# An mLSTM and attention trunk on one core: earlier down weights in the second MLP, and GpSimd sharing the conditioning sums

## The chip, the cores and the metric

The kernel runs on one core of a Trainium2 chip. The core has a matrix engine (TensorE, PE in the profile; its weight loads are listed as PEld), VectorE (DVE), ScalarE (ACT), GpSimd (POOL) and SyncE (SP), whose queue issues the transfers of this kernel. The metric is the device time of one execution in microseconds, as the median of several runs. Before the change it is 2478.76 us (three runs, 2478.34 to 2480.81).

## The reference

The reference is one inference step of a two-layer trunk over a prompt of 1024 rows and a sample of 32 rows, each 1024 wide. Both go through the same weights with their own state and their own conditioning vector `c`. Cut to what matters here:

```
def ada_mod(c, w, b):
    return jax.nn.silu(c) @ w + b
...
for l in range(DEPTH):                      # DEPTH = 2
    sh1, sc1, g1, sh2, sc2, g2 = split(ada_mod(c, w_ada[l], b_ada[l]), 6)
    u = x * (1 + sc1) + sh1
    y = mlstm_mixer(u, ...) if l == 0 else band_attention(u, ...)
    x = layer_norm(ALPHA * x + (1 + g1) * y)
    u = x * (1 + sc2) + sh2
    f = square(relu(u @ w_up[l])) @ w_down[l]     # 1024 -> 4096 -> 1024
    x = layer_norm(ALPHA * x + (1 + g2) * f)
```

So each layer needs six vectors of 1024 conditioning values, for two conditioning vectors (that of the prompt and that of the sample), and a further pair of vectors feeds the shared keys and values. Each is a product of a vector of 1024 with a matrix of 1024 columns. All results are float32. The kernel reaches that accuracy on PE by splitting each operand into a high part and the rest, and by three matmuls for each product (high by high, high by rest, rest by high).

## The kernel before, in words

Prompt and sample rows lie side by side as 1056 columns, in three blocks of 384, 384 and 288. Stage after stage, PE does the products: the first conditioning values and the mLSTM's projections with the mLSTM itself, up to about 480 us; the first MLP, up to about 1260; queries, keys, values and attention, up to about 1640; the output projection; the second MLP from about 1720 to the end. The kernel is written with a library that plans, from the order of the program and from estimated durations, in which order the instructions of an engine stand in its queue, and that puts in the waits. Two stretches have PE's order written out by hand: attention and the down stage of the second MLP (`manual_schedule`). An engine, SyncE among them, works through its queue in order.

The conditioning sums. The first 2048 columns of layer 0 are done on PE. All others are done by `ada_cols`, in pairs of 128-column blocks: `ada_l0` (16 pairs) runs beside the mLSTM, `ada_rest` (24 pairs of layer 1 and 8 for keys and values) beside the first MLP. A pair reads its weights in two halves (line 231), each with four chunks of 128 rows; for each chunk and each of the two vectors (`cnd` 0 and 1) VectorE multiplies 128x256 weights by one value per partition and adds the product to the sum `acc[:, cnd]` (line 238; the first one writes without adding, line 241). Then it transposes the sums (line 245), reduces them over 32 columns (line 246), and after each fourth pair PE finishes the sum over partitions. `ada_l0` has a single buffer, `ada_room`, with places for one half of the weights, for the sums and for the transposed sums; `ada_rest` takes its weights from the ring of three "raw" buffers that also receives the weights of the MLP (line 96), and its sums from the ring of five temporaries (`tmp_t`). The generators are fed forward by `flow.tick`, a few ticks per step, so that these sums lie among the other work.

The second MLP (`mlp7`). Its up stage runs in 16 blocks of 256 hidden columns. Blocks 0 to 13 are prepared for a product with fewer multiplications: each pair of quarters of the 1056 columns becomes seven operands, written to memory (`hd`, line 1170). Blocks 14 and 15 (`NW` and `NW + 1`) are taken plainly by `up_plain`: relu and square on ACT, the split into an `hl` tile, which is written to memory too (`hpl`, line 1191) for a last plain stage. For block 15 the `hl` tiles come from a pool of two buffers; for block 14 they come from the ring of three raw buffers.

The down stage then works in 16 units (four groups of blocks by four blocks of 256 output columns). A unit needs weights in seven forms, which `forms` makes from two loads (`rdn`, line 1228) into raw buffers, split and summed on ACT and VectorE (lines 89, 90, 1245 to 1248), and 14 operands `fx`, which `fill` reads back from `hd` into free rooms (line 1117). Rooms are four tiles `f4` at first; when block 15's up products no longer read one half of the MLP's input, that half's memory gives further rooms (`L.rooms(tp0)`, then `tp1`). `prep(i)` asks for the weights of unit `i`; each `next(preps[i])` makes one step of its forms. The order of the program between the up and the down stage is, before the change: rooms and the first operands, `up_plain` of block 14, `prep(0)`, `up_plain` of block 15's first half, the four steps of unit 0's forms, `prep(1)`, rooms and operands, `up_plain` of the second half, rooms and operands, and then the units, by hand, on PE (line 1283), with VectorE adding each result (line 986).

Of the kernel before, what the change touches and what calls it, by code (L numbers as in the profile page):

```python
# [9 lines left out]
F32R = mybir.dt.float32r  # L10
AF = mybir.ActivationFunctionType
ALU = mybir.AluOpType
# [3 lines left out]
P = 128  # L16
# [59 lines left out]
def trunk_kernel(ctx: ExitStack, tc: tile.TileContext, a, o):  # L76
    nc = tc.nc
# [3 lines left out]
    ring = ctx.enter_context(tc.tile_pool(name="ring", bufs=1, reuse_waits="tile"))  # L81
# [5 lines left out]
    def split(dst_h, dst_l, src, eng=None):  # L87

        nc.scalar.copy(dst_h, src)
        (eng or nc.vector).tensor_sub(dst_l, src, dst_h.bitcast(F32))  # L90
# [74 lines left out]
    def ada_part(l, i):  # L165
        return ada[:, l * 48 + i * KC:l * 48 + (i + 1) * KC, :]
# [10 lines left out]
    def tpt(name):  # L177
        return pa.tile([P, 512], F32, tag="tp", name=name, bufs=2)
# [27 lines left out]
    tp = tpt("tp_c")  # L206
# [13 lines left out]
    tp = tpt("tp_p2")  # L220
# [3 lines left out]

    def ada_cols(src, c0, base, nch, mk, tmp_f, step, raw_f=raw_tile):

        for j in range(0, nch, 2):
            acc = tmp_f([P, 2, 256], f"aacc_{base}_{j}")
            for half in range(2):
                raw = raw_f([P, 4, 256], f"rada_{base}_{j}_{half}")  # L230
                nc.sync.dma_start(raw, src[512 * half:512 * half + 512, c0 + j * P:c0 + (j + 2) * P].rearrange(
                    "(k p) c -> p k c", p=P))
                yield step[0]
                for k in range(4):
                    for cnd in range(2):
                        sc = cs[:, 4 * half + k, cnd:cnd + 1]
                        if half or k:
                            nc.vector.scalar_tensor_tensor(acc[:, cnd], raw[:, k], sc, acc[:, cnd],  # L238
                                                           op0=ALU.mult, op1=ALU.add)
                        else:  # L240
                            nc.vector.tensor_scalar(acc[:, cnd], raw[:, k], sc, None, op0=ALU.mult)
                    if k == 1 and step[1]:
                        yield step[1]
            at = tmp_f([P, 512], f"aat_{base}_{j}")
            nc.vector.transpose(at, acc.rearrange("p c n -> p (c n)"))
            nc.vector.tensor_reduce(out=cx[:, j // 2 % 4], in_=at.rearrange("p (b i) -> p b i", i=32), axis=mybir.AxisListType.X,
                                    op=ALU.add)
            yield step[2]
            if j // 2 % 4 == 3:
                ps = mk(f"adas_{base}_{j}")  # L250
                for q in range(4):
                    nc.tensor.matmul(ps[32 * q:32 * q + 32, :16], sel, cx.rearrange("p g b -> p (g b)")[:, q::4],
                                     start=True, stop=True)
                b0 = base + j - 6
                nc.vector.tensor_tensor(
                    ada[:, b0:b0 + 8, :].rearrange("p (g b) c -> p g b c", g=4),
                    ps[:, :16].rearrange("p (g c b) -> p g b c", g=4, c=2),
                    pt2[:, b0:b0 + 8].rearrange("p (g b) -> p g b", g=4)[:, :, :, None].broadcast_to([P, 4, 2, 2]),
                    op=ALU.add)

    def ada_fix(base, parts):

        for i, kind in parts:
            ap = ada[:, base + i * KC:base + (i + 1) * KC, :]
            if kind == "sc":
                nc.vector.tensor_scalar_add(ap, ap, 1.0)
            else:
                nc.vector.tensor_scalar(ap, ap, 1.0, 1.0 / ALPHA, op0=ALU.add, op1=ALU.mult)
# [461 lines left out]
    def ada_l0():  # L730
        room = ring.tile([P, 2112], F32, tag="wc", name="ada_room", bufs=6)

        def raw_f(shape, name):
            return room[:, 1024:2048].rearrange("p (k c) -> p k c", k=4)

        def tmp_f(shape, name):
            return room[:, 512:1024] if len(shape) == 2 else room[:, :512].rearrange("p (k c) -> p k c", k=2)
        yield from ada_cols(a["w_ada"][0], 2048, 16, 32, adat, tmp_f, ADA_C, raw_f)
        ada_fix(0, [(2, "g"), (4, "sc"), (5, "g")])
    flow.add(ada_l0())  # L740
# [56 lines left out]
    def tmp_t(shape, name, dt=F32):  # L797
        return T_.tile(shape, dt, tag="t", name=name, bufs=5)
# [290 lines left out]
    QN = T // 4  # L1089
    NPB, KG = 16, 4  # L1090
    NW = 14
# [32 lines left out]
    def mlp7(L):  # L1124
# [7 lines left out]
        l, mm = L.l, L.alloc  # L1132
# [14 lines left out]
        def up_mm(pb, f, q):  # L1147
            ps = mm(f"up{l}_{pb}_{f}_{q}")
            proj(ps[:, :QN], QN, up_w(pb), f, lambda hl, k: L.u(hl, k, q))
            return ps[:, :QN]  # L1150
# [29 lines left out]
        def up_plain(pb, tp):  # L1180
            for f in range(2):
                r = tmp_t([P, 2, QN], f"hr{l}_{pb}_{f}_{tp}")
                for i in range(2):
                    nc.scalar.activation(r[:, i], up_mm(pb, f, 2 * tp + i), AF.Relu)
                    flow.tick(QN / 96)
                nc.scalar.activation(r, r, AF.Square)
                name = f"hl{l}_{pb}_{f}_{tp}"
                hl = hlp.tile([P, 2, 2, QN], F32R, tag="hl", name=name, bufs=2) if pb == NPB - 1 else \
                    ring.tile([P, 2, 2, QN], F32R, tag="raw", name=name, bufs=3)
                split(hl[:, 0], hl[:, 1], r)  # L1190
                nc.sync.dma_start(hpl[2 * (pb - NW) + f, :, :, 2 * tp * QN:2 * (tp + 1) * QN],
                                  hl.bitcast(F32).rearrange("p l q t -> p l (q t)"))

        tp0, tp1 = L.pairs
# [24 lines left out]
        hlp = hl_cm.__enter__()  # L1219
# [75 lines left out]
        def prep(i):  # L1295
            if i < len(units):
                preps[i] = forms(*units[i][:2], f"{l}_{i}")
                next(preps[i])
        for t in f4:
            rooms.add(t)  # L1300
        want += [(tp, f) for tp in L.pairs for f in order_f]
        fill(0, fx)
        for tp in L.pairs:
            up_plain(NW, tp)
        prep(0)
        up_plain(NW + 1, tp0)
        for _ in range(4):
            got[0] = next(preps[0])
        prep(1)
        for t in L.rooms(tp0):  # L1310
            rooms.add(t)
        fill(0, fx)
# [53 lines left out]
    acc_cm, acc = open_acc(0, fwd)  # L1366
    mm, norm, _, out_proj, mlp, _, _ = make_layer(acc, bank, uap)
# [286 lines left out]
    with tc.manual_schedule(engines={mybir.EngineType.PE}):  # L1654
        for gp in range(2):
            for i in range(17):
                c = slim[gp][i // 2] if i % 2 else wide[i // 2] if i < 16 else slim[gp][8]
# [18 lines left out]
    acc = {ti: ACC[:, :, t0:t0 + n] for ti, (t0, n) in enumerate(TBS)}  # L1676
# [12 lines left out]
    def u2ap(hl, k, t0, n):  # L1689
# [5 lines left out]
    mm, norm, norm_out, out_proj, _, gain_shift, add_gated_at = make_layer(  # L1695
        acc, lambda name: psD.tile([P, 512], F32, tag="mm", name=name, bufs=8), u2ap, 2 * QN)
# [25 lines left out]
    class L1:  # L1722
        wups = wup1
        l, alloc, add, gate = 1, mm, add_gated_at, ada_part(1, 5)
# [74 lines left out]
```

## Time and profile before

| | |
|---|---|
| median of three runs | 2478.76 us (2478.34 to 2480.81) |
| the profiled execution | 2479.81 us, span 2478.0 us |
| PE busy | 2413.7 us, 97% of the span |
| VectorE busy | 1759.7 us, 71% |
| ScalarE busy | 1016.9 us, 41% |
| GpSimd busy | 168.6 us, 7% |
| mean granted clock of PE | 0.992 of full speed |

The profile is taken from one execution, by the chip. An instruction has the line of the program that issued it; many are issued by helpers, so that lines 118 to 120 are the matmuls of every plain product, and lines 89 and 90 the two halves of every split. Names such as `dn<-fx,wf` say which tile is written from which. "Idle before" is the time that an engine stood still just before an instruction, with what released it.

### The profile page before, as it was taken

Reading aid. Unit: us, or ns where it says so; the run is one execution under the profiler, and the core shown is the slowest. Engines: PE = TensorE matmul, PEld = TensorE weight load, DVE = VectorE, ACT = ScalarE, POOL = GpSimd, SP = SyncE. Lnnn points to the kernel's source line nnn. Section 1 sums busy time; section 2 is a strip of 40 time slices with the busy share of each in tenths; the row PEclk is TensorE's granted clock in tenths of the full one; section 3 lists DMA queues with packets and bytes.
Section 4 is the critical chain, followed back from the end, with each engine's and each line's share of the span. In section 5 each row is a group of like instructions: output and inputs, shape, how many; then the busy total and the mean of one; then the engine's idle time right before and its main releaser. Section 6 shows DMA issues by size and latency. Waiting matters only on the chain.

```text
span 2478.0 us, 42688 instructions
## 1 busy us (share of the span) xinstructions
PE 2413.7 (97%) x16844; PEld 2315.4 (93%) x16844; DVE 1759.7 (71%) x4038; ACT 1016.9 (41%) x2118; POOL 168.6 (7%) x315
## 2 busy tenths in 40 slices
PE   7999999999999999999999999999999999999997
PEld 4999999999999999999999867789999999899997
DVE  4899999788679679677597667746853442776758
ACT  4644456382211212212266556654754443221212
POOL 0211100000000000000001134410000000000003
PEclk9999999999999999999999989999999999999999
DMA  8433224313224224234122310050375646767632
GB/s 297 122 110 101 84 88 129 107 35 119 77 87 137 84 86 135 80 92 142 43 98 82 91 40 1 18 147 27 134 251 212 215 179 254 262 239 273 255 130 72
DMA packets 236220, 318.10 MB, mean 128 GB/s; under 512 B 11624, under 2 KB 185084, under 8 KB 234996
## 3 DMA queue, kind: packets, MB, share of 16 engines
q1 hardware_dynamic: 236020, 315.38, 38.8%
q8 instruction: 132, 2.16, 0.4%
q14 instruction: 68, 0.56, 0.1%
HBM read 242.79 MB, written 74.91 MB: 128 GB/s over the span
## 4 chain that ended last, share of the span: by engine, by line
PE 78%; DVE 8%; DMA 6%; ACT 2%; issue 1%; POOL 0%; SPq 0%; DVEq 0%; POOLq 0%; ACTq 0%
PE up L118 10%; PE up L120 10%; PE up L119 9%; PE dn L1283 9%; PE dn L119 5%; PE dn L118 5%; PE dn L120 5%; DMA fx<-hd 3%; PE pv L1608 2%; PE pt L1588 2%; PE s L1558 2%; PE o L118 1%; PE o L119 1%; PE o L120 1%; PE op_b L118 1%
## 5 line engine op out<-in xcount | busy, mean ns | idle before, releaser
L120 PE MATMUL up<-u,w_up 128*128 128x264 f32 x1024 | 292.9, 286 | 0.0
L118 PE MATMUL up<-u,w_up 128*128 128x264 f32 x1024 | 292.4, 286 | 0.0
L119 PE MATMUL up<-u,w_up 128*128 128x264 f32 x1024 | 291.1, 284 | 0.0
L1283 PE MATMUL dn<-fx,wf 128*128 128x264 f32 x2208 | 275.3, 286 | 7.9 <-DMA fx<-hd 7.4
L1283 PEld LDWEIGHTS dn<-fx,wf 128*128 128x128 f32 x2208 | 272.2, 189 | 9.7 <-issue 4.6
L119 PE MATMUL dn<-h,w_dn 128*128 128x384 f32 (+1 forms) x768 | 249.5, 325 | 0.0
L118 PE MATMUL up<-U,w_up 128*128 128x384 f32 (+1 forms) x768 | 249.2, 324 | 0.0
L119 PE MATMUL up<-U,w_up 128*128 128x384 f32 (+1 forms) x768 | 247.9, 323 | 0.0
L118 PE MATMUL dn<-h,w_dn 128*128 128x384 f32 (+1 forms) x768 | 247.8, 323 | 0.0
L120 PE MATMUL up<-U,w_up 128*128 128x384 f32 (+1 forms) x768 | 247.6, 322 | 0.0
L120 PE MATMUL dn<-h,w_dn 128*128 128x384 f32 (+1 forms) x768 | 247.3, 322 | 0.0
L119 PEld LDWEIGHTS up<-u,w_up 128*128 128x128 f32 x1024 | 193.9, 189 | 0.0
L118 PEld LDWEIGHTS up<-u,w_up 128*128 128x128 f32 x1024 | 193.8, 189 | 0.0
L120 PEld LDWEIGHTS up<-u,w_up 128*128 128x128 f32 x1024 | 193.3, 189 | 0.0
L986 DVE SCALAR_TENSOR_TENSOR ACC<-dn,ada,ACC 128x264 f32<-128x264 f32 (+4 forms) x328 | 131.7, 426 | 86.4 <-PE dn L1283 74.6
L238 DVE SCALAR_TENSOR_TENSOR aacc<-rada,cs,aacc 128x256 f32<-128x256 f32 x448 | 190.3, 477 | 0.0
L986 DVE SCALAR_TENSOR_TENSOR acc<-dn,ada,acc 128x384 f32<-128x384 f32 (+2 forms) x256 | 119.4, 486 | 47.4 <-PE dn L120 46.3
L1025 ACT ACTIVATE r<-up 128x384 f32<-128x384 f32 (+1 forms) x96 | 44.3, 463 | 246.9 <-PE up L120 238.4
L119 PEld LDWEIGHTS dn<-h,w_dn 128*128 128x128 f32 x768 | 144.4, 188 | 0.2 <-DVE h L1028 0.2
L120 PEld LDWEIGHTS dn<-h,w_dn 128*128 128x128 f32 x768 | 144.5, 188 | 0.0
L120 PEld LDWEIGHTS up<-U,w_up 128*128 128x128 f32 x768 | 144.3, 188 | 0.0
L118 PEld LDWEIGHTS up<-U,w_up 128*128 128x128 f32 x768 | 144.2, 188 | 0.1
(354 smaller groups left out, 5957.4 us busy)
## 6 DMA issues: line engine op xcount, KB each, us to landing
hd<-HL SPq DMA_DIRECT2D x28, 1848.0 KB
raw_up<-in_w_up_dram SPq DMA_DIRECT2D x68, 512.0 KB
rada<-in_w_ada_dram SPq DMA_DIRECT2D x64, 512.0 KB
fx<-hd SPq DMA_DIRECT2D x37, 528.0 KB
raw_dn<-in_w_down_dram SPq DMA_DIRECT2D x36, 512.0 KB
ada_room<-in_w_ada_dram SPq DMA_DIRECT2D x32, 512.0 KB
fx<-hd SPq DMA_DIRECT2D x50, 264.0 KB
fx<-hd SPq DMA_DIRECT2D x16, 792.0 KB
```

What stands on the lines that cost most here:

```text
L118: nc.tensor.matmul(ps, wh, mov(0, k), start=(k == 0), stop=False)
L119: nc.tensor.matmul(ps, wh, mov(1, k), start=False, stop=False)
L120: nc.tensor.matmul(ps, wl, mov(0, k), start=False, stop=(k == nk - 1))
L238: nc.vector.scalar_tensor_tensor(acc[:, cnd], raw[:, k], sc, acc[:, cnd], op0=ALU.mult, op1=ALU.add)
L986: nc.vector.scalar_tensor_tensor(xs, ps[:, off + o:off + o + mm_], gate[:, fc, cnd:cnd + 1], xs, op0=ALU.mult, op1=ALU.add)
L1025: nc.scalar.activation(r, ps[:, :n], AF.Relu)
L1283: nc.tensor.matmul(p, ws[w][:, wl, k], t[:, s0, xl], start=first and k + n_ == 0, stop=k == kg - 1 and n_ == 2, skip_group_check=not first)
L1558: nc.tensor.matmul(s[:, b, :w], qst, kk[i][:, g, k0 + j0:k0 + j0 + w], start=(i == 0), stop=(i == 1))
L1588: nc.tensor.transpose(pt[:kp, j - j0, pr * P:(pr + 1) * P], ps_[pr][:, j * P:j * P + kp], ident)
L1608: nc.tensor.matmul(pv[64 * e:64 * e + 64, :nq], V[:kp, vt0 + j, g * 64:(g + 1) * 64], pts[e][:kp, j, :nq], start=(j == 0), stop=(j == nt - 1))
```

## The change

It has three edits. In `ada_cols` the products and sums of the second vector (`cnd` 1, the sample's) go to GpSimd; since GpSimd is given no instruction that multiplies and adds, each is a product into a tile of its own (`apr`) and an addition. In the mLSTM `apr` lies where the transposed sums lie; in the first MLP it is a temporary. In `up_plain` all `hl` tiles come from the pool of two buffers. In `mlp7` `prep(0)` moves ahead of the rooms and the first operands, and the four steps of unit 0's forms and `prep(1)` move ahead of `up_plain` of block 15's first half.

```diff
@@ ada_cols
                 for k in range(4):
                     for cnd in range(2):
                         sc = cs[:, 4 * half + k, cnd:cnd + 1]
-                        if half or k:
+                        if cnd:
+                            pr = tmp_f([P, 256], f"apr_{base}_{j}_{half}_{k}") if half or k else acc[:, 1]
+                            nc.gpsimd.tensor_scalar(pr, raw[:, k], sc, 0.0, op0=ALU.mult, op1=ALU.add)
+                            if half or k:
+                                nc.gpsimd.tensor_add(acc[:, 1], acc[:, 1], pr)
+                        elif half or k:
                             nc.vector.scalar_tensor_tensor(acc[:, cnd], raw[:, k], sc, acc[:, cnd],
                                                            op0=ALU.mult, op1=ALU.add)
                         else:
@@ ada_l0
         def tmp_f(shape, name):
-            return room[:, 512:1024] if len(shape) == 2 else room[:, :512].rearrange("p (k c) -> p k c", k=2)
+            return room[:, 512:512 + shape[1]] if len(shape) == 2 else room[:, :512].rearrange("p (k c) -> p k c", k=2)
@@ mlp7, up_plain
-                name = f"hl{l}_{pb}_{f}_{tp}"
-                hl = hlp.tile([P, 2, 2, QN], F32R, tag="hl", name=name, bufs=2) if pb == NPB - 1 else \
-                    ring.tile([P, 2, 2, QN], F32R, tag="raw", name=name, bufs=3)
+                hl = hlp.tile([P, 2, 2, QN], F32R, tag="hl", name=f"hl{l}_{pb}_{f}_{tp}", bufs=2)
@@ mlp7
+        prep(0)
         for t in f4:
             rooms.add(t)
         want += [(tp, f) for tp in L.pairs for f in order_f]
         fill(0, fx)
         for tp in L.pairs:
             up_plain(NW, tp)
-        prep(0)
-        up_plain(NW + 1, tp0)
         for _ in range(4):
             got[0] = next(preps[0])
         prep(1)
+        up_plain(NW + 1, tp0)
         for t in L.rooms(tp0):
             rooms.add(t)
         fill(0, fx)
```

## The prediction, made before the result was known

> **What bounds the kernel now.** I read the page first, then who waited for whom on TensorE (PE), stretch by stretch, and then the order of time around the one place where PE waits long.
>
> ```profile
> span 2478.0 us, 42688 instructions
> PE 2413.7 (97%) x16844; PEld 2315.4 (93%) x16844; DVE 1759.7 (71%) x4038; ACT 1016.9 (41%) x2118; POOL 168.6 (7%) x315
> L1283 PE MATMUL dn<-fx,wf 128*128 128x264 f32 x2208 | 275.3, 286 | 7.9 <-DMA fx<-hd 7.4
> ```
>
> PE sets the end: 97% busy. An edit elsewhere counts only where it moves a wait of PE. The second MLP's down stage (L1283) has such waits, and they lie close together. Windows of 25 us, whose columns are the length, the busy time and count of PE, PEld, DVE, ACT, POOL, the clock, the DMA share and GB/s:
>
> ```profile
> 2075.00:2100.00 25.00, 25.00 (x207) 25.00 (x207) 4.99 (x6) 10.99 (x21) 0.00 (x0) 1.00 0.82 297
> 2100.00:2125.00 25.00, 22.11 (x176) 21.29 (x174) 17.11 (x38) 9.84 (x22) 0.00 (x0) 1.00 0.96 354
> 2125.00:2150.00 25.00, 22.11 (x161) 21.65 (x162) 15.90 (x37) 4.11 (x8) 0.00 (x0) 0.86 0.87 308
> 2150.00:2175.00 25.00, 25.00 (x208) 25.00 (x207) 19.24 (x44) 6.01 (x12) 0.00 (x0) 1.00 0.51 167
> ...
> 2110.23 1.99 PE L1283 MATMUL dn<-fx,wf 128*128 128x264 f32 x15
> 2119.66 1.73 PE L1283 MATMUL dn<-fx,wf 128*128 128x264 f32 x12 [0.23 <-DMA fx<-hd]
> 2123.35 1.00 PE L1283 MATMUL dn<-fx,wf 128*128 128x264 f32 x6 [1.96 <-DMA fx<-hd]
> 2127.49 2.32 PE L1283 MATMUL dn<-fx,wf 128*128 128x264 f32 x9 [3.15 <-DMA fx<-hd]
> 2130.11 6.14 PE L1283 MATMUL dn<-fx,wf 128*128 128x264 f32 x37 [0.29 <-DMA fx<-hd]
> ```
>
> Undisturbed, 25 us hold 208 matmuls, one per 0.120 us. The two disturbed windows hold 337 where 416 fit: 79 are missing, 9.5 us. Of these 5.63 us are the four bracketed waits for operands fx; the rest is the clock granted after them, 0.86 in the second window. So 9.5 us is all that this place can give.
>
> Why are the operands late? SyncE's queue (SPq: start, time to the last issue, what):
>
> ```profile
> 2084.24 6.59 SPq L1117 DMA_DIRECT2D fx<-hd  x7
> 2091.06 0.52 SPq L1191 DMA_DIRECT2D hpl<-hl  x1
> 2092.92 1.04 SPq L1228 DMA_DIRECT2D rdn<-in_w_down_dram  x2
> 2095.35 6.38 SPq L1191 DMA_DIRECT2D hpl<-hl  x2
> 2103.71 4.49 SPq L1228 DMA_DIRECT2D rdn<-in_w_down_dram  x2
> 2108.26 4.20 SPq L1117 DMA_DIRECT2D fx<-hd  x8
> 2115.06 8.58 SPq L1117 DMA_DIRECT2D fx<-hd  x6
> ...
> 2098.71 0.39 ACT L1184 ACTIVATE hr<-up 128x264 f32<-128x264 f32 x1 [2.52 <-PE up L120]
> 2104.68 0.51 ACT L89 CAST wf<-rdn 128x384 fp32r<-128x384 f32 x1 [4.25 <-DMA rdn<-in_w_down_dram]
> ...
> 2107.21 0.55 DVE L1247 TENSOR_TENSOR s<-rdn 128x384 f32<-128x384 f32 x1
> ```
>
> The second batch of operands (x8) goes into the memory of half of the MLP's input, which PE has read for the last time when ACT takes its last tile at 2098.71. It is issued at 2108.26, 9.5 us later: in the queue ahead of it stands the second of unit 1's weight loads (2103.71, x2), which needs a "raw" buffer that only unit 0's sums (DVE L1247 at 2107.21) give back. Unit 0's weights were asked for at 2092.92, behind the first operands and behind four hl tiles that held the same three raw buffers, and were read at 2104.68. Meanwhile the transfers are near their limit (share 0.96).
>
> **The change, part by part.** *Second MLP.* All hl tiles now take two buffers of their own; unit 0's weights are first in the program, and its forms and unit 1's weights come before the up products of the last block's first half. The raw buffers are last used by the up weights:
>
> ```profile
> 2041.47 1.22 DVE L90 TENSOR_TENSOR w_up<-raw_up,w_up 128x1024 fp32r<-128x1024 f32 x1 [0.53 <-ACT w_up L89]
> ```
>
> so three are free from 2042.7, and four loads of 384 KB can leave before 2084. (If unit 1's second load still waits on L1247, that now runs as soon as unit 0's weights land.) The x8 can then go at about 2099, the x6 at about 2112, after PE's last up product at 2110.2. From 2084.24 there remain 14 operands of 792 KB and six hl writes of 528 KB, 14.6 MB; at the 354 GB/s of the busy window they end 41.2 us later, at 2125.4. PE, starting at 2110.23 with 126 matmuls (15.2 us), wants the last operand 1.1 us before 2125.4. So 1.1 us of wait is left and 9.5 - 1.1 = **8.4 us are saved**. Ends: 9.5, and 0 if another entry of the queue holds the operands as long. Two hl buffers in place of three and two: a tile is made from 48 matmuls, so each 5.8 us, and written from the queue; behind a late buffer stand ACT's relus, but eight PSUM banks cover some 20 us of up products. I take nothing. What is late next moves along with PE: the later waits for fx sum to 7.4 - 5.6 us.
>
> *Conditioning sums.* `ada_cols` is one function, so its three uses all change: 16 column pairs in the mLSTM and 32 in the first MLP. Per pair GpSimd gets 8 products and 7 sums of 128x256 and VectorE loses as many. GpSimd's prices stand in other stages, VectorE's in place:
>
> ```profile
> L1574 POOL TENSOR_SCALAR p<-p,mx 128x256 f32<-128x256 f32 x8 | 3.8, 482 | 7.1 <-DVE mx L1573 6.1 <-PE s L1558 0.9
> L1487 POOL TENSOR_TENSOR x<-x,kvss 128x256 f32<-128x256 f32 x1 | 0.6, 621 | 5.5 <-DMA x<-xsp 5.5
> ...
> L238 DVE SCALAR_TENSOR_TENSOR ada_room<-ada_room,cs x224: 452/476/1023, 70.9 to 448.0; 128x256 f32<-128x256 f32 x112
> ...
> L238 DVE SCALAR_TENSOR_TENSOR aacc<-rada,cs,aacc x448: 468/477/484, 567.0 to 1148.2; 128x256 f32<-128x256 f32 x150
> ...
> 445.23 3.26 DVE L238 SCALAR_TENSOR_TENSOR ada_room<-ada_room,cs 128x256 f32<-128x256 f32 x8
> ...
> 100.00:450.00 350.00, 345.23 (x2263) 327.47 (x2261) 320.09 (x930) 179.76 (x479) 37.35 (x105) 1.00 0.36 110
> 460.00:1250.00 790.00, 789.91 (x4943) 787.40 (x4942) 589.48 (x1243) 223.43 (x383) 0.00 (x0) 1.00 0.29 89
> ```
>
> GpSimd: 8 x 0.482 + 7 x 0.621 = 8.2 us a pair, 131 us in the mLSTM and 262 us in the first MLP. VectorE in a row needs 3.26/8 = 0.41 us for each, so the mLSTM frees 128 x 0.41 = 52 us and the first MLP 105 us. But the two engines hold each other up:
>
> ```profile
> 333.47 0.48 POOL L619 TENSOR_TENSOR qc<-y,rc 128x128 f32<-128x128 f32 x1 [5.70 <-PE num L632]
> ...
> 333.53 0.70 DVE L238 SCALAR_TENSOR_TENSOR ada_room<-ada_room,cs 128x256 f32<-128x256 f32 x1
> ```
>
> VectorE's sum, 0.48 us otherwise, took 0.70 beside GpSimd's product: it started effectively at 333.75, so GpSimd was in the way until 0.2 us before its end. Less 0.2 each, GpSimd's 240 operations of the mLSTM hold VectorE off for at most 128 x 0.28 + 112 x 0.42 = 83 us. My estimate is that six in ten of that meets an instruction that reads two SBUF tiles (sums, convolution, splits are over half of its work there): 50 us, against 52 freed. VectorE's load stays at 320 of 350 us, and PE's small waits on it stay: 0.
>
> The Trainium skill's page "SBUF — State Buffer", section "Who interferes with whom", says that a VectorE instruction with two SBUF inputs and a GpSimd instruction that reads SBUF exclude each other, the later one blocked until the other finishes. The row of 0.70 us agrees that it blocks, and ends the block 0.2 us early.
>
> PE's waits in the mLSTM, and the end of its chain:
>
> ```profile
> PE op_a L118 <- ACT w_oa L89: 2.0, 1, 2.0
> PE cu L634 <- DVE hn L660: 1.6, 2, 1.0
> PE S L612 <- DVE y L561: 0.9, 1, 0.9
> ...
> 431.33 0.37 SPq L231 DMA_DIRECT2D ada_room<-in_w_ada_dram  x1
> 441.14 0.37 SPq L231 DMA_DIRECT2D ada_room<-in_w_ada_dram  x1
> 441.61 1.57 SPq L96 DMA_DIRECT2D raw_oa<-in_w_out_a_dram  x1
> ```
>
> Here a sum is on the path: there is one `ada_room`, so its next load (441.14) waits for the last sum of the half, and the output projection's weights (441.61), for which PE waits 2.0 us at 450.7, stand behind. A half takes GpSimd 4 x (0.482 + 0.621) = 4.41 us in place of 3.26: +1.15. Two halves run back to back before 441.61: **+2.3 us**. Ends: -2.0 if the planner now puts the weights ahead, +5.8 if five halves add up.
>
> GpSimd's queue is passed too: qc (L619), which PE's next chunk needs, can stand behind a half's 4.4 us. The row at 333.47 shows GpSimd idle 5.70 us for a buffer before it, so a qc is made at least a chunk ahead: nothing, and up to 4.4 us a chunk without that lead. First MLP: PE never waits there (789.91 of 790 us); a pair comes every (1148.2 - 567.0)/32 = 18 us, for GpSimd's 8.2. The slower halves hold raw buffers 1.15 us longer ahead of weight loads; covered, I take nothing, nor for the products' temporaries (about 1.1 us each, out of the ring of five that the up stage shares). Uncovered it is 64 x 1.15 = 74 us.
>
> Sum: -8.4 + 2.3 = -6.1. The profiled execution took 2479.81 us (span 2478.0 and 1.8 around it), 1.05 above the median of the runs: 2473.7 in its terms, **2472.7** in the median's.
>
> **The rivals.** (1) *The waits of the mLSTM go as well*: the weights get ahead of the sums (-2.0) and VectorE, freed, no longer holds PE (-2.5 of the rows above): 2478.8 - 8.4 - 4.5 = 2466. For it: VectorE at 91%, the busiest helper. Against: the 0.70 us. (2) *The operands stay late*: transfers near 0.96 are the real limit, the early loads only swap places, or an hl write blocks the queue. Gain 0 to 3: with +2.3, 2479. For it: the share; against: before 2100 the share is 0.82, so there is room, and 9.5 us of queue are lost to one entry. (3) *Slower: VectorE blocked in the mLSTM*. Freed 52 plus idle 30 us (350 - 320) bear 82 us of blocking; from there PE waits for hn, splits and the convolution. At the full 131 us it costs 49 us; at 100 it costs 18: 2478.8 - 8.4 + 18 = 2488. For it: VectorE's load; against: the hold ends early, and many of its operations read PSUM. The skill's rule, blocking to the finish, would give up to 131 us, so it speaks for this one.
>
> **How the numbers follow.** Forecast 0.50, rival 1 0.17, rival 2 0.15, rival 3 0.18. What a measurement can tell from no change is about 0.2%, 5 us: faster is below 2473.8. Of the forecast about two thirds lie there (0.34), with rival 1 0.51; same: 0.16 + 0.15 + 0.02 of rival 3 = 0.33; slower 0.16. Range 2464 (rival 1 and all 9.5 us) to 2486 (rival 3 begun); the forecast's own is 2468 to 2477.
>
> **What would show it.** In the changed profile: rdn loads ahead of the first fx; x8 at about 2099 less the shift so far; no wait of over 1.5 us on fx at unit 0, no clock dip; POOL about 394 us longer; L238 of DVE halved to 336; VectorE's load between 100 and 450 within 20 us of 320; op_a's wait 2 to 6 us. I am wrong if PE's start of the second down stage has moved by more than 6 us either way, or if the fx waits persist with the loads in the new order.

## The result, and the profile after

| | before | after |
|---|---|---|
| median | 2478.55 us (2477.12 to 2481.08, six runs) | 2570.44 us (2568.11 to 2571.14, six runs) |
| the profiled execution | 2479.81 us, span 2478.0 us | 2570.94 us, span 2569.1 us |
| mean granted clock of PE | 0.992 | 0.978 |

The ratio is 1.0368, with a 95% interval of 1.0354 to 1.0381. The change makes the kernel slower by 92 us; the prediction was 6 us faster, 2464 to 2486, and it was wrong. From the page of after, the engines, the second MLP's down stage, and the instructions that the conditioning sums have in the first MLP:

```profile
PE 2441.1 (95%) x16844; PEld 2338.9 (91%) x16844; DVE 1735.1 (68%) x3654; ACT 1017.4 (40%) x2118; POOL 701.4 (27%) x1035
L1287 PE MATMUL dn<-fx,wf 128*128 128x264 f32 x2208 | 277.3, 287 | 6.8 <-DMA fx<-hd 6.5
...
L242 POOL TENSOR_TENSOR aacc<-aacc,apr 128x256 f32<-128x256 f32 x224 | 192.7, 860 | 7.0
...
L240 POOL TENSOR_SCALAR apr<-rada,cs 128x256 f32<-128x256 f32 x224 | 153.5, 693 | 46.5 <-DVE h L1034 45.6
L244 DVE SCALAR_TENSOR_TENSOR aacc<-rada,cs,aacc 128x256 f32<-128x256 f32 x224 | 151.3, 675 | 4.1
```

GpSimd is busy for 533 us more, not 394, and VectorE, which gave up half of its sums, is busy for only 25 us less. PE's down stage of the second MLP waits for fx almost as long as before (6.5 us, 7.4 before).

Where do the 92 us arise? The view of one tile gives the first and the last start of its matmuls (minimum, median and maximum length in ns stand before them). The last product of `o` closes the mLSTM's share of PE, the last of `op_a` the output projection behind it. Before:

```profile
L120 PE MATMUL o<-U,w_o x192: 292/336/423, 305.9 to 417.3; 128*128 128x384 f32 x128, 128*128 128x288 f32 x64
L120 PE MATMUL op_a<-U,w_oa x192: 293/336/342, 418.1 to 515.0; 128*128 128x384 f32 x128, 128*128 128x288 f32 x64
```

After:

```profile
L120 PE MATMUL o<-U,w_o x192: 291/336/522, 357.3 to 491.2; 128*128 128x384 f32 x128, 128*128 128x288 f32 x64
L120 PE MATMUL op_a<-U,w_oa x192: 293/336/522, 492.1 to 603.5; 128*128 128x384 f32 x128, 128*128 128x288 f32 x64
```

So 73.9 us (417.3 to 491.2) are lost in the mLSTM and 14.6 more at the step to the output projection; 88.5 of the 91.1 us of the span are gone by 603.5. PE matmuls and VectorE in that stretch, in the order of the columns of the prediction's windows, before:

```profile
60.00:418.00 358.00, 352.27 (x2346) 333.68 (x2344) 326.65 (x929) 195.48 (x507) 41.88 (x112) 1.00 0.34 102
```

After:

```profile
60.00:492.00 432.00, 374.07 (x2348) 351.60 (x2348) 315.97 (x816) 196.40 (x509) 188.74 (x308) 0.94 0.28 83
```

For the same matmuls PE stands idle for 58 us in place of 6, and its busy time grows by 22 us. The granted clock goes from 1.00 to 0.94 with it, and 352.27 / 0.94 is 375 us, near the 374.07 that were measured. VectorE is not full: it is busy for 316 of 432 us, 73%, where it was 91%. It waits. The waits of PE between 60 and 570 us, after (in all, times, longest; before, that of cu for hn was 1.6 us and that of ae_ps for stk 2.2 us):

```profile
PE cu L640 <- DVE hn L666: 30.0, 12, 5.9
PE ae_ps L529 <- ACT stk L522: 10.1, 1, 10.1
PE op_a L118 <- ACT w_oa L89: 9.1, 1, 9.1
...
PE adas L258 <- DVE cx L252: 3.8, 1, 3.8
```

The waits of VectorE for the room up to the end of `o`, before, when none of them was for GpSimd:

```profile
DVE ada_room L241 <- DMA ada_room<-in_w_ada_dram: 4.1, 3, 3.0
...
DVE ada_room L238 <- DMA ada_room<-in_w_ada_dram: 3.2, 2, 1.6
```

After:

```profile
DVE ada_room L244 <- DMA ada_room<-in_w_ada_dram: 20.4, 8, 5.4
DVE ada_room L251 <- POOL ada_room L242: 19.5, 9, 3.4
```

VectorE works through its queue in order. Its sums wait for the next load of the room, which may not start until GpSimd has read the last one; its transposition waits for GpSimd's last sum; and hn, on which PE waits, stands behind both. (`num` and `cu` share two buffers. `hn` is the last to read a `num`, and the next `cu` takes its buffer.) One such place, VectorE first and then PE:

```profile
205.39 0.71 DVE L251 STREAM_TRANSPOSE ada_room<-ada_room 128x512 f32<-128x512 f32 x1 [2.55 <-POOL ada_room L242]
...
208.10 0.55 DVE L666 TENSOR_SCALAR hn<-num,sm 128x256 f32<-128x256 f32 x1
...
208.80 1.20 PE L640 MATMUL cu<-vt,kw 128*128 128x257 f32 x2 [4.95 <-DVE hn L666]
```

Another one, on VectorE, at the gates of the mLSTM:

```profile
79.66 0.48 DVE L244 SCALAR_TENSOR_TENSOR ada_room<-ada_room,cs 128x256 f32<-128x256 f32 x1 [5.35 <-DMA ada_room<-in_w_ada_dram]
...
86.76 0.71 DVE L251 STREAM_TRANSPOSE ada_room<-ada_room 128x512 f32<-128x512 f32 x1 [3.44 <-POOL ada_room L242]
...
90.26 2.27 DVE L499 TENSOR_TENSOR_SCAN mr<-tt,ig 4x1024 f32<-4x1024 f32 x1
...
100.63 0.69 DVE L521 TENSOR_SCALAR tt<-mr 4x1056 f32<-4x1056 f32 x1
```

The scan and its successors make the gates. They stand behind 8.8 us of waits that did not concern them (5.35 + 3.44). ACT writes the gates' rows (stk) from tt, at 101.4 us where it did at 93.9 before, and PE's transposes ae_ps wait 10.1 us for that.

What the sums take now, by tile (ns: shortest, median, longest; first and last start):

```profile
L240 POOL TENSOR_SCALAR ada_room<-ada_room,cs x128: 474/532/3094, 70.8 to 542.1; 128x256 f32<-128x256 f32 x128
L244 DVE SCALAR_TENSOR_TENSOR ada_room<-ada_room,cs x112: 447/582/1253, 71.2 to 539.4; 128x256 f32<-128x256 f32 x112
L242 POOL TENSOR_TENSOR ada_room<-ada_room x112: 719/763/1853, 72.1 to 542.7; 128x256 f32<-128x256 f32 x112
```

And GpSimd's by group, with the mean behind the busy time:

```profile
L242 POOL TENSOR_TENSOR ada_room<-ada_room 128x256 f32<-128x256 f32 x112 | 94.2, 841 | 8.9
L240 POOL TENSOR_SCALAR ada_room<-ada_room,cs 128x256 f32<-128x256 f32 x128 | 90.7, 710 | 147.2 <-DMA ada_room<-in_w_ada_dram 60.6 <-DVE ada L272 50.5 <-DVE cx L252 14.6
```

A half (the four chunks of one load) takes GpSimd 4 x (0.710 + 0.841) = 6.2 us, where the prediction had 4.41. VectorE's sum has a median of 582 ns, where it had 476.

The second MLP: the weights were asked for early (2130.84; PE's up products lie 89.9 us later there than before, so this is 2041 on the clock of before), and yet the operands came no sooner. Of the four loads that the prediction had leave before 2084, these two did; the third left at 2181.35, 2091.5 on the clock of before. SyncE's queue, after:

```profile
2130.84 2.13 SPq L1232 DMA_DIRECT2D rdn<-in_w_down_dram  x2
...
2170.25 8.51 SPq L1123 DMA_DIRECT2D fx<-hd  x7
2179.80 1.23 SPq L1195 DMA_DIRECT2D hpl<-hl  x2
...
2182.21 0.73 SPq L1123 DMA_DIRECT2D fx<-hd  x1
2193.20 1.18 SPq L1195 DMA_DIRECT2D hpl<-hl  x2
...
2201.78 3.38 SPq L1123 DMA_DIRECT2D fx<-hd  x5
```

Its waits between 2165 and 2225:

```profile
SPq L1195 <- DVE hl L90: 14.3, 3, 9.6
```

ACT's first cast into an hl tile:

```profile
2178.40 1.17 ACT L89 CAST hl<-hr 128x528 fp32r<-128x528 f32 x2 [1.15 <-DMA hd<-HL]
```

The first hl tile is cast only at 2178.4: the cast waits for the store of the last results of the blocks before (hd from HL). The first two tiles are then written at 2179.80, behind seven operands. The third and fourth take the same two buffers again, and the queue stands for up to 9.6 us at their write (2193.20), until they are made. That they were made so late because of the buffers is argued, not shown: in ACT's queue their casts were planned behind other work, and only two later casts wait for a buffer itself, 3.2 us in all. The eight operands (x8) that were one batch at 2108.26 now leave between 2182.21 and 2205.2, five of them from 2201.78, which is 2111.9 on the clock of before.

### The profile page after: what moved, and what is told of

Read it like the earlier page. It is cut to its first block, busy times and chain, and to the rows that moved or that the text cites. A ratio compares the mean times of both kernels' runs of the same rounds, so it can differ in the third digit from the quotient of the medians.

```text
span 2569.1 us, 43132 instructions
## 1 busy us (share of the span) xinstructions
PE 2441.1 (95%) x16844; PEld 2338.9 (91%) x16844; DVE 1735.1 (68%) x3654; ACT 1017.4 (40%) x2118; POOL 701.4 (27%) x1035
## 4 chain that ended last, share of the span: by engine, by line
PE 73%; DVE 9%; DMA 8%; POOL 6%; issue 2%; ACT 2%; SPq 0%; POOLq 0%; DVEq 0%; ACTq 0%
PE up L118 10%; PE up L120 9%; PE up L119 9%; PE dn L1287 9%; PE dn L119 5%; PE dn L118 5%; PE dn L120 5%; DMA ada_room<-in_w_ada_dram 3%; DMA fx<-hd 3%; POOL ada_room L240 3%; POOL ada_room L242 2%; PE pv L1612 2%; PE pt L1592 2%; PE s L1562 2%; PE op_b L118 1%
## 5 line engine op out<-in xcount | busy, mean ns | idle before, releaser
L977 POOL TENSOR_TENSOR yb<-yb,gb 128x512 f32<-128x512 f32 (+1 forms) x14 | 20.2, 1456 | 816.2 <-DVE yb L976 816.2
L242 POOL TENSOR_TENSOR aacc<-aacc,apr 128x256 f32<-128x256 f32 x224 | 192.7, 860 | 7.0
L240 POOL TENSOR_SCALAR apr<-rada,cs 128x256 f32<-128x256 f32 x224 | 153.5, 693 | 46.5 <-DVE h L1034 45.6
L244 DVE SCALAR_TENSOR_TENSOR aacc<-rada,cs,aacc 128x256 f32<-128x256 f32 x224 | 151.3, 675 | 4.1
```

Of the source, the lines that this page charges most:

```text
L240: nc.gpsimd.tensor_scalar(pr, raw[:, k], sc, 0.0, op0=ALU.mult, op1=ALU.add)
L242: nc.gpsimd.tensor_add(acc[:, 1], acc[:, 1], pr)
```

## The experiments

All are made from the kernel before, except where another is named. Each median stands against runs of before on the same chip, whose medians lay between 2478.1 and 2479.8 us.

**Which part costs.** Four kernels, each with a part of the change: the condition `if cnd:` of `ada_cols` is narrowed to one of its uses, or the edits of `mlp7` and `up_plain` are taken alone.

```diff
 # e1: the mLSTM alone (e2: base != 16, the first MLP alone; e3: mlp7 and up_plain alone; e4: both uses)
-                        if cnd:
+                        if cnd and base == 16:
```

> The kernel before with GpSimd taking the sample's sums in the mLSTM alone (ada_l0); the first and second MLP as before. Theory A (nearly all of the loss is made in the mLSTM, whose output projection ended 74 us later, op_a 88 us later): 2478.5 + 88 = 2566, within 6 us. Rival B (the loss is a sum over all stages, because GpSimd and VectorE hinder each other wherever the sums lie; a third of the operations are in the mLSTM): about 2510.

Measured: 2566.62 us, ratio 1.0354 (1.0338 to 1.0369).

> The kernel before with GpSimd taking the sample's sums in the first MLP alone (ada_rest), twice as many operations as in the mLSTM. Theory A: PE never waits there, 2478 to 2481. Rival B: about 2540, two thirds of the loss.

Measured: 2481.78 us, ratio 1.0010 (1.0001 to 1.0020).

> The kernel before with the edits of the second MLP alone (early weights of the first down units, all hl tiles from two buffers), conditioning sums as before. Theory A (the wait moved from the raw buffers to the two hl buffers and the operands are no earlier in effect): 2478 to 2480, no difference. Rival C (my prediction's term holds without the sums and was hidden by the later parts of the changed kernel): 2470.

Measured: 2480.16 us, ratio 1.0009 (0.9999 to 1.0019).

> The kernel before with GpSimd's sums in both places and the second MLP as before. Theory A: the sum of the first two runs, about 2568; the difference to the whole change (2570.4) is that of the second MLP's edits, 0 to 2 us.

Measured: 2570.49 us, ratio 1.0366 (1.0347 to 1.0385).

What follows: 88 of the 92 us belong to the mLSTM alone. In the first MLP twice as many of the same instructions cost about 3 us (by the interval 0 to 5), though there too GpSimd and VectorE slow each other (693, 860 and 675 ns in the rows above): of PE's waits there, only one is on VectorE, 0.9 us in the trace of the whole change. Even the 3 us are not all from there. In the trace of e2 the last product of op_a, ahead of the first MLP, already starts 1.7 us later than before (516.7 against 515.0). The second MLP's edits bring nothing.

**What it is in the mLSTM.** A ladder from "the sample's sums left out" to GpSimd's sums as in e1. In e5, e6, e7, e9, e13 and e14 the sample's sums of layer 0 are not in the result.

```diff
 # e5: left out
-                    for cnd in range(2):
+                    for cnd in range(1 if base == 16 else 2):
 # e6: and beside it, for each chunk, into a spare tile from the constant tile cs
+                        nc.gpsimd.tensor_scalar(spare, csf, cs[:, 4 * half + k, 1:2], 0.0, op0=ALU.mult, op1=ALU.add)
+                        if half or k:
+                            nc.gpsimd.tensor_add(spare, spare, csf)
 # e7: as e6, but the product reads the room
-                        nc.gpsimd.tensor_scalar(spare, csf, cs[:, 4 * half + k, 1:2], 0.0, op0=ALU.mult, op1=ALU.add)
+                        nc.gpsimd.tensor_scalar(spare, raw[:, k], cs[:, 4 * half + k, 1:2], 0.0, op0=ALU.mult, op1=ALU.add)
```

> The kernel before; in the mLSTM the sample's products and sums are left out altogether (its sums are a constant zero), so VectorE does half of the sums and GpSimd none; the sample's conditioning of layer 0 is missing from the result. First step of a ladder to the 2566.6 us of GpSimd's sums in the mLSTM. Both theories: VectorE is freed of some 52 us and nothing else happens: 2474 to 2478, since PE's waits on VectorE there sum to 2.5 us.

Measured: 2486.29 us, ratio 1.0032 (1.0023 to 1.0042): slower than before, although VectorE has less to do. No one had expected that. VectorE's waits for the room's loads up to the end of `o` grew from 7.3 to 16.5 us, and PE's last product of `o` starts at 424.7 in place of 417.3. The planner put VectorE's instructions into quite another order. Which part of the 8 us is due to what was not tried.

> As the run before, but GpSimd issues as many products and sums of the same shape at the same places, from a constant tile into a spare tile: nothing waits for them and they wait for nothing, so the two engines can hinder each other only through the memory and GpSimd's own queue (qc and others behind the sums). The sample's conditioning of layer 0 is missing from the result. Theory A (the loss comes from VectorE standing in order behind waits for GpSimd's sums and for the single room): 2476 to 2490. Rival P (the engines exclude each other at the memory; my third rival): most of the 88 us, 2530 to 2566.

Measured: 2583.25 us, ratio 1.0423 (1.0404 to 1.0441). Its number lies above even rival P's range, and its trace shows that it is neither theory. PE's waits:

```profile
PE ae_ps L530 <- ACT stk L523: 62.2, 1, 62.2
PE qk L118 <- ACT qkp L551: 22.0, 1, 22.0
```

GpSimd's sums, tied to nothing, ran one after another from 5 us on, and its fill of stk and its copies into qkp stood behind them in its queue. It was an experiment on the order of GpSimd's queue, not on the memory.

> As the run before, but GpSimd's products read the weights in the room, so each load of the room waits for GpSimd too; VectorE's transposition still does not wait for GpSimd (results go into the spare tile). The sample's conditioning of layer 0 is missing from the result. Theory A in its first form (the transposition standing in order behind GpSimd's last sum is what costs): no more than 10 us above the run before. Theory A in its second form (the later loads, for which VectorE's sums wait in order, cost most): over half of the 88 us appears here.

Measured: 2553.38 us, ratio 1.0303 (1.0286 to 1.0319). VectorE's waits for the room's loads, up to the end of `o`:

```profile
DVE ada_room L241 <- DMA ada_room<-in_w_ada_dram: 20.4, 9, 5.4
DVE ada_room L244 <- DMA ada_room<-in_w_ada_dram: 14.1, 9, 3.7
```

It is 67 us above e5, more than half of the 88, as the second form of theory A had it. But e6, on which it was to stand, is no base, and GpSimd's reading is in it as well as its hold of the room. So e7 alone does not tell the two apart.

> The run in which GpSimd's sums were tied to nothing (2583.3 us) could not answer its question: GpSimd ran all of them early, and its memory fill for stk and its copies for qkp, for which PE waited 62 and 22 us, stood in its queue behind them. Here the same products and sums (constant tile to spare tile) are held to their places: the first product of a first half reads one value of the previous pair's result, that of a second half one value of VectorE's sum. They don't hold the room's weights, and nobody waits for them. The sample's conditioning of layer 0 is missing from the result. Base: 2486.3 us with the sums left out. Theory A (hold of the room and order of VectorE's queue): 2486 to 2500. Rival P (the engines hinder each other at the memory): 2530 to 2553.

Measured: 2544.98 us, ratio 1.0262 (1.0237 to 1.0286). That speaks for rival P; but the value of VectorE's sum that paced GpSimd made VectorE wait 14.2 us for GpSimd in turn, so the run was made again without it.

```diff
 # e13: one product of a pair reads the result of the pair before
+                        pace = cs[:, 4 * half + k, 1:2] if half or k else cx[:, (j // 2 - 1) % 4, 15:16]
+                        nc.gpsimd.tensor_scalar(spare, csf, pace, 0.0, op0=ALU.mult, op1=ALU.add)
 # e14: and all behind it are fills
+                            for _ in range(5):
+                                nc.gpsimd.memset(spare, 0.0)
```

> As the paced run (2545.0 us), but only the first product of a pair is held, by one value of the pair before; no value of VectorE's running sum is read, so VectorE never waits for GpSimd. What is left is what the engines do to each other at the memory, and GpSimd's own queue. The sample's conditioning of layer 0 is missing from the result. Base: 2486.3 us with the sums left out. If waits in VectorE's queue are most of it: 2488 to 2500. If the memory is most of it: 2515 to 2545.

Measured: 2548.05 us, ratio 1.0279 (1.0265 to 1.0293): 3 us above the range for the memory, and far from that for the waits.

> As the run above, with GpSimd's products and sums (after the first of a pair) replaced by fills of the spare tile that take about as long, which write the memory and don't read it. GpSimd's queue is as full, the reading is gone. If the run above is slow through reading beside VectorE's two-operand instructions: here 2484 to 2492, and VectorE's busy time back from some 350 to about 323 us. If it is slow through GpSimd's queue (copies and qc behind the sums): the same time as above.

Measured: 2514.84 us, ratio 1.0141 (1.0126 to 1.0157). Neither range is met: 33 us of e13's loss go with the reading, and 35 us against before stay.

Why so much stays is in the trace. Behind `o`, SyncE's loads of acc wait 24.2 us for GpSimd's last use of the spare tile, and the output projection's last weights stand behind them in the queue. In e13 this wait is 16.9 us and in e7 10.4. The change and e1 have no such wait, it is the experiment's own. So these kernels are compared by the last product of `o`, which lies ahead of it.

The window of e5 up to the end of `o`, whose last product starts at 424.7:

```profile
60.00:425.00 365.00, 357.09 (x2347) 336.93 (x2345) 293.91 (x818) 195.49 (x508) 35.40 (x112) 0.99 0.34 101
```

The last row of the view of `o`, and the window up to its end, of e14:

```profile
L120 PE MATMUL o<-U,w_o x192: 291/336/588, 316.0 to 433.5; 128*128 128x384 f32 x128, 128*128 128x288 f32 x64
```

```profile
60.00:434.00 374.00, 361.39 (x2351) 340.40 (x2349) 296.26 (x820) 195.96 (x509) 178.72 (x544) 0.98 0.33 99
```

Of e13:

```profile
L120 PE MATMUL o<-U,w_o x192: 292/336/421, 343.1 to 461.6; 128*128 128x384 f32 x128, 128*128 128x288 f32 x64
```

```profile
60.00:462.00 402.00, 363.59 (x2360) 341.65 (x2358) 316.81 (x824) 197.68 (x513) 171.56 (x292) 0.97 0.31 93
```

GpSimd is busy for about as long in e13 and e14 (172 and 179 us), and in the two traces VectorE's and PE's instructions stand in the same order, so the plan is no rival here. Where GpSimd also reads, VectorE's nearly equal work takes 316.8 us. Where it only fills, the work takes 296.3, against 293.9 without GpSimd's sums. And with the reading `o` ends 28 us later (461.6 against 433.5). VectorE's sums make it plain, by groups, of e13 and then of e14:

```profile
L241 DVE SCALAR_TENSOR_TENSOR ada_room<-ada_room,cs 128x256 f32<-128x256 f32 x105 | 59.9, 571 | 7.5 <-DMA ada_room<-in_w_ada_dram 6.9
```

```profile
L241 DVE SCALAR_TENSOR_TENSOR ada_room<-ada_room,cs 128x256 f32<-128x256 f32 x112 | 54.6, 487 | 11.5 <-DMA ada_room<-in_w_ada_dram 10.4
```

The Trainium skill's page "SBUF — State Buffer", section "Who interferes with whom", says that a VectorE instruction with two SBUF inputs contends with a GpSimd instruction that reads SBUF, and not with one that only writes it. The 571 and 487 ns agree.

In e13 nobody waits for the results of GpSimd's sums and the room is not held by it. VectorE is busy for 317 of 402 us, 79%. Still PE's wait for hn is

```profile
PE cu L642 <- DVE hn L668: 22.2, 14, 6.5
```

where the kernel before had 1.6 us and e14 has 5.9. So VectorE need not be full for PE to wait: 20 us of lengthening (296.3 to 316.8), spread over its queue, are enough.

The ladder by the last product of `o`. From e14 to e13 the order of VectorE and PE is the same, so 28 us are the reading's. It is also the same in e5 and e7, so the three steps between them add up to 49 us without the plan's help. The other steps change the planner's order too, whose own effect may be the 7 us of e5. (e9, in another order and with more waits than e13, ended `o` 9 us sooner.) So each of those is good to some 10 us:

| kernel | what is added | last `o`, us | step |
|---|---|---|---|
| before | | 417.3 | |
| e5 | sample's sums taken from VectorE | 424.7 | +7.4 |
| e14 | GpSimd's queue full, almost no reading | 433.5 | +8.8 |
| e13 | GpSimd reads memory beside VectorE | 461.6 | +28.1 |
| e7 | the room held by GpSimd | 474.0 | +12.4 |
| e1 | the transposition waits for GpSimd | 491.0 | +17.0 |

**The share of the hold, and other ways to share.**

```diff
 # e11 (GpSimd as in e1) and e12 (VectorE alone): quarters of 256 KB, two places, the next load ahead of the sums
-            return room[:, 1024:2048].rearrange("p (k c) -> p k c", k=4)
+            return room[:, 1024 + 512 * i:1536 + 512 * i].rearrange("p (k c) -> p k c", k=2)
 # e15: e11 and
+            yield 1.0
             at = tmp_f([P, 512], f"aat_{base}_{j}")
 # e10: GpSimd takes columns n: of the sample
+                        n = 192 if cnd and base == 16 else 256
```

> GpSimd's sums in the mLSTM as in the change (2566.6 us alone), with the room's place for weights cut in two: quarters of 256 KB, the next one asked for ahead of the sums of this one. The load is then no longer exposed between the sums of two halves. Theory A: VectorE's waits for ada_room's load fall from some 26 us to under 10 and over half of the loss goes: 2490 to 2525. Rival P: 2555 to 2567.

Measured: 2531.67 us, ratio 1.0214 (1.0188 to 1.0240). 35 of the 88 us go, less than half. VectorE's waits up to the end of `o` fall. In e1 they are

```profile
DVE ada_room L250 <- POOL ada_room L241: 20.7, 9, 3.4
DVE ada_room L243 <- DMA ada_room<-in_w_ada_dram: 18.7, 8, 5.5
```

and in e11

```profile
DVE ada_room L299 <- POOL ada_room L290: 12.7, 8, 3.6
...
DVE ada_room L292 <- DMA ada_room<-in_w_ada_dram: 8.6, 8, 2.5
```

The ranges of neither theory are met. The waits are a part of the loss, and the planner's order has changed as well. This run does not divide the 53 us that remain.

> The kernel before, VectorE doing all sums, with the room's place for weights cut in two as in the run above (64 loads of 256 KB for 32 of 512 KB). Theory A: the waits for the loads (9.7 us of VectorE before) go, and PE's waits for it with them: 2474 to 2478. Rival Q (the shorter loads and more entries in the queue cost more than they bring): over 2481.

Measured: 2484.63 us, ratio 1.0023 (1.0013 to 1.0033). This is rival Q's range. Without GpSimd the two places cost 6 us, so they are no gain in themselves. The 35 us of e11 come off what GpSimd's sums cost.

> The kernel before, with GpSimd taking 64 of the 256 columns of the sample's sums in the mLSTM and VectorE the other 192 and the prompt's 256. GpSimd's half is then shorter than VectorE's, so it is never the one that holds the room; its instructions are as many as in the change (240), and VectorE's as many as before. Theory A: 2476 to 2486. Rival P, by instructions: as much as the change, 2550 to 2566; by columns: a quarter of it, about 2500.

Measured: 2500.87 us, ratio 1.0079 (1.0050 to 1.0107). The number is that of rival P by columns. GpSimd's products and sums of 64 columns still take 0.556 and 0.406 us on average, so its half, 3.8 us, is no shorter than VectorE's, 4 x (0.508 + 0.437) = 3.8. Yet in the trace the waits for GpSimd are gone: up to the end of `o` VectorE's transposition waits 1.3 us for it (in e1 20.7), and the room's next load waits for VectorE's sums, and not for GpSimd's products, on which it waited 42 us in e1. `o` ends 15 us later than before all the same (432.2). That speaks for the memory, but the order was planned anew here too.

> GpSimd's sums with the two places for weights (2531.7 us), with one more step of the surrounding work between the last sum and VectorE's transposition. In that run VectorE stood 15.3 us behind GpSimd's sums at the transposition. If waits in VectorE's queue cost PE about as much as they last: 2515 to 2522. If not: 2528 to 2534.

Measured: 2538.43 us, ratio 1.0242 (1.0228 to 1.0256), above both ranges. The transposition still waited 16.3 us for GpSimd: the step later in the program did not put more between the two in time. What that wait costs by itself stays with the ladder's 17 us.

**The second MLP's operands.**

```diff
-        prep(1)
         for t in L.rooms(tp0):
             rooms.add(t)
         fill(0, fx)
+        prep(1)
```

> The kernel before with one thing moved: the request for unit 1's weights in the second MLP stands behind the operands that go into the first freed half of the input. My prediction's term for the second MLP (9.5 us of the queue are lost to that one entry, at most 9.5 us of PE to be had): the eight operands issue at about 2102 in place of 2108.3 and the time falls by 5 to 8 us, to about 2472. Rival D (the transfers are at their limit anyway): 2478, the waits for fx only change places.

Measured: 2477.54 us, ratio 0.9994 (0.9981 to 1.0006).

> The kernel before with unit 1's weights asked for behind the operands, once more: its trace gained 2.8 us at that place (the lag of PE's matmuls against before went from -6.1 to -8.9 us over unit 0), its median 0.6 us. Theory (the transfers were at their full share, 1.03, so freeing the queue 6 us earlier gives only 2 to 3 us): 2475 to 2477. Rival: no gain, 2478 to 2480.

Measured: 2477.87 us, ratio 0.9992 (0.9983 to 1.0001). In the first of the two, the queue's batch, PE's first down products, and the windows around them:

```profile
2095.65 6.97 SPq L1117 DMA_DIRECT2D fx<-hd  x8
```

```profile
2104.10 11.13 PE L1283 MATMUL dn<-fx,wf 128*128 128x264 f32 x90
```

```profile
2075.00:2100.00 25.00, 25.00 (x207) 25.00 (x206) 3.86 (x7) 8.89 (x17) 0.00 (x0) 1.00 1.03 374
2100.00:2125.00 25.00, 20.85 (x156) 19.99 (x154) 17.66 (x40) 9.23 (x20) 0.00 (x0) 0.93 1.04 397
2125.00:2150.00 25.00, 24.93 (x204) 24.93 (x205) 20.07 (x47) 5.45 (x11) 0.00 (x0) 1.00 0.66 228
```

The eight operands leave 8.4 us ahead of the down stage, against 2.0 before. 56 matmuls are missing from the two disturbed windows (416 - 360) in place of 79, a gain of 23, or 2.8 us. (The stage as a whole starts 6.1 us sooner than before in this execution, by differences ahead of the edit.) The transfers are at a share of 1.03 and 1.04 from 2075 to 2125. In the trace of e16 the operands leave 8.4 us ahead as well, 59 matmuls are missing, a gain of 2.4 us, and the share between 2100 and 2125 is 1.05. The medians are 0.6 and 1.9 us ahead of before, which is less than can be told from no change. Of all the edits tried it is the only one that is not behind.

## Why the prediction was wrong

- *Conditioning sums in the mLSTM: "VectorE's load stays at 320 of 350 us, and PE's small waits on it stay: 0."* This is the step that failed, by 74 us. The load came out near, 316 us of busy time for the work that took 327 (spread over 74 us more, so the window from 100 to 450 holds 266), but by luck: over the whole execution VectorE is busy for 1759.7 us before, 1722.0 in e5 and 1749.4 in e1, so the sums that leave it free some 38 us, not 52, and GpSimd takes some 27 back, not 50. The conclusion from the load failed: PE's idle time, for which the sum had 0 more, went from 6 to 58 us, and 22 us of lower clock came on top. PE's wait for hn was 1.6 us before, which reads as if hn came just in time, in an order planned for it; how early each hn came is not shown. What counts is how late a single hn is, not how full VectorE is. The third rival had the hold at the memory, which the runs show, and a wrong point from which it decides: 82 us of blocking, the room until VectorE is full. The runs show it deciding long before: 20 us of lengthening (296.3 in e14 to 316.8 in e13) put the end of `o` 28 us back.
- *The size of the hold.* I estimated 50 us for VectorE; its lengthening up to the end of `o` is 22 us (293.9 in e5 to 316.0 in the change, for nearly equal instructions). GpSimd's side had no term at all, and is the larger: against the shortest ones of the run (474 and 719 ns), 128 x (0.710 - 0.474) + 112 x (0.841 - 0.719) = 44 us. The row of a single VectorE instruction that was held up was taken for the whole. The rows of the change show GpSimd's instructions lengthened too.
- *GpSimd's price of 0.621 for a sum* stood on one row, of another tile. The shortest here is 0.72 us. With the hold a half is 6.2 us, in place of 4.41.
- *The wait that was not in the list.* Of the new waits I asked what stands behind GpSimd's sums in GpSimd's queue (qc: rightly nothing, PE waits for no qc). I did not ask what stands in VectorE's queue behind VectorE's waits for GpSimd: the transposition, and the sums that now wait for a room held longer. The +1.15 us a half was counted where two halves run back to back, at the end, and not at the 30 other halves. By the ladder the two together are 29 of the 74 us, good to some 10, since the planner's order changed with them.
- *Step to the output projection, +2.3, ends -2.0 and +5.8.* Right in kind, 14.6 us in fact: the wait of op_a for its weights is 9.1 us, where 2 to 6 were to show it, and one for adas of 3.8 us comes to it. The halves take 6.2 us, and more of them are left over: the room's last sum starts at 542.7, 52 us behind the last product of `o`, where it started at 448.0, 31 us behind it.
- *First MLP: "covered, I take nothing".* Near enough: some 3 us for 480 instructions.
- *Second MLP, -8.4.* Wrong twice. "Two hl buffers in place of three and two ... I take nothing" failed: the wait for the stored results and then the writes of the hl tiles put the operands behind them where the weights had been. And the term itself was too large: with the queue free 6 us earlier (e8) the place gives 2.8 us, where 8.4 were forecast. The transfers read as the limit then, at a share of 1.03 and 1.04. Both halves of the second rival are seen, the entry that blocks and the share near its end. I had set the share of 0.82 before 2100 against it. What counted is the window behind it, which is at 1.04 once the queue is free.

## What to carry to other kernels

An engine's busy share does not price work that is taken from it or given to it where another engine waits for single results of it: ask by how much that result is early now, and if the trace already shows short waits for it, as the two of 1 us at most here, take it as not early at all. When a loop is split over two engines that share a buffer or a result, list what stands in order behind each new wait on both, and price the hold of the buffer at the slower engine's time, with both engines slowed by each other. The same split cost 88 us where PE waited on VectorE and some 3 us, with twice the instructions, where it hardly did.

## What the runs showed of the hardware that was not expected

GpSimd's reading beside VectorE lengthens both: VectorE's sum of 128x256 from a median of 476 to one of 582 ns in the mLSTM, and from 477 to a mean of 675 in the first MLP; GpSimd's product from 474 at the shortest to a mean of 710, and its sum from 719 to 841. Fills that keep GpSimd as busy leave VectorE's sum at a mean of 487. PE's idle time is paid for a second time: in the mLSTM the same matmuls took 374 in place of 352 us, with the granted clock at 0.94 in place of 1.00. The windows above show it in steps: with 6, 8, 13, 38 and 58 us of idle time (before, e5, e14, e13, the change) the granted clock is 1.00, 0.99, 0.98, 0.97 and 0.94.
